# The third part of the gate-weighted one-hot rows made on ScalarE, four scaled copies per step, in a hybrid decoder layer

## The chip, the cores and the metric

One core of a Trainium2 chip runs one launch of the kernel. The metric is the device time of that launch in microseconds (us). The engines are TensorE (PE; its weight loads are shown apart as PEld), VectorE (DVE), ScalarE (ACT), GpSimd (POOL) and SyncE (SP), whose queue issues most transfers. Each engine takes its instructions in order; semaphores order them across engines.

## The reference, cut to what matters

The layer is a pooling mixer and latent attention, then a product-key expert retrieval over 128 x 128 experts for 512 tokens of width 1024. The change lies in the retrieval:

```python
s1, i1 = lax.top_k(sc[:, :, 0], PEER_TOPK)
s2, i2 = lax.top_k(sc[:, :, 1], PEER_TOPK)
cand = (s1[..., :, None] + s2[..., None, :]).reshape(TOK_CHUNK, PEER_HEADS, PEER_TOPK * PEER_TOPK)
cidx = (i1[..., :, None] * PEER_NKEYS + i2[..., None, :]).reshape(TOK_CHUNK, PEER_HEADS, PEER_TOPK * PEER_TOPK)
s, j = lax.top_k(cand, PEER_TOPK)
idx = jnp.take_along_axis(cidx, j, axis=-1)
gate = jax.nn.softmax(s, axis=-1)
u = peer_u[idx]
a = jax.nn.gelu(jnp.einsum('thkd,td->thk', u, xc).astype(jnp.float32), approximate=False)
w = (gate * a).astype(xc.dtype)
return jnp.einsum('thk,thkd->td', w, peer_v[idx])
```

Each token takes 128 experts (8 heads of 16), each named by a row number i1 and a column number i2, and weighs it by a gate.

## The kernel before, in words

The tokens are four tiles of 128. Three of them (`DT = 3`) go the dense way: for all 16384 experts, in 128 blocks of 128, the kernel forms `gelu(u x)`, multiplies by a gate matrix G that is zero for experts a token did not choose, and multiplies by v. The fourth tile gathers its experts row by row in a later stage.

G is built in the **G stage**, by `g_tiles()`. For each dense token tile `g_prep(t)` turns the list of i1, i2 and gates so that the 128 choices lie on partitions and tokens along the free axis (three PE transposes, three ScalarE copies). The gate is split into three bf16 parts, so that their sum is the fp32 gate. Then `g_tiles()` goes through the tokens four at a time: 32 steps for a token tile, 96 in all, counted by `q`. A step has these parts, in the order in which they are written:

- L1099, DVE: tile `o` of step q gets the one-hot rows of i2 and i1, for four tokens (a 128x1024 bf16 comparison).
- L1103, DVE: in the tile of step q-1, parts 2 and 3 of the output rows, as the product of the one-hot row `o[:, 1]` with two of the gate parts (128x1024 bf16).
- L1104, DVE: the same with the remaining part, in place over `o[:, 1]` (128x512 bf16).
- L1111, PE: for step q-4 (`LL = 4`), 12 matmuls of 128x128 into one PSUM tile `gp`, which has four buffers.
- L1116, ACT: for step q-5, the PSUM tile is copied to `stg`; every fourth copy is followed by a transfer to `Gd`.
- a share of `top_second(t+1)`, small DVE operations that find the choices of the next token tile (in the first two token tiles only). At step 29 of a token tile what is left of it is run out and `g_prep` of the next one follows.

Between the steps `beside()` runs `u_part()`, 2.4 times a step (`R_G` times `KD`). It makes the blocks `u x`: eight parts of three matmuls to a block (L196 to L198 in `mm3`), so a block starts every 3.33 steps. At the start of a block `u_parts()` issues the gelu of the block before (L845, ACT, waits for that block's last matmul) and then `weights()`, which splits the u block that comes next but one into a high and a low part: L208, ACT, makes the high part (128x1024), and L205, DVE, takes the difference and so waits for L208:

```python
        act.activation(hi, src, AF.Copy)
        low(lo, src, hi, eng)
```

The order on each engine is the order in which the code is written; nothing reorders it. So on DVE, L205 stands after the products of the step that has just been issued, and L1099 and L1103 of the next step stand behind it.

Of the kernel before, what the change touches and what calls it, by code (L numbers as in the profile page):

```python
# [11 lines left out]
BF = mybir.dt.bfloat16  # L12
I32 = mybir.dt.int32
U32 = mybir.dt.uint32
AF = mybir.ActivationFunctionType
# [5 lines left out]
P = 128  # L21
# [32 lines left out]
N_BACK = 36  # L54
# [95 lines left out]
def trace(ctx: ExitStack, tc: tile.TileContext, A, out):  # L150
    nc = tc.nc
    ctx.enter_context(tc.manual_schedule())
    act, dve, pe, pool, sync = nc.scalar, nc.vector, nc.tensor, nc.gpsimd, nc.sync
# [6 lines left out]
    def stage(name, space=None):  # L160
        kw = {"space": space} if space else {}
        st = stages.enter_context(ExitStack())
        return st, st.enter_context(tc.tile_pool(name=name, bufs=1, **kw))

    pools = {}
# [3 lines left out]
    BUFS = {"S2": N_S2, "F": N_F, "H": 4, "G": 2, "s": 8, "sm": 16, "sr": 1, "sa": 4}  # L169
    uid = [0]  # L170

    def T(tag, shape, dt=F32):
        uid[0] += 1
        return pools.get(tag, cpool).tile(list(shape), dt, name=f"{tag}_{uid[0]}", tag=tag, bufs=BUFS[tag])
# [4 lines left out]
    def wide(dt=F32, shape=(P, D)):  # L179
        return T("F", shape, dt)  # L180
# [90 lines left out]
    one = cpool.tile([P, 1], F32, name="one")  # L271
# [408 lines left out]
    scale = (NOPE + ROPE) ** -0.5  # L680
# [283 lines left out]
    sb_main, main = stage("sb_main")  # L964
    pools["B"] = main
    sb_top, pools["sm"] = stage("sb_top")
    pools["sm2"] = pools["gp3"] = pools["bt"] = pools["sm"]
    ps_g, psg = stage("ps_g", PSUM)
    BUFS.update(B=N_BACK, W=4, sm2=2, gp3=2, bt=2, Y=1)
    sel = {}  # L970

    def top_second(t):
# [87 lines left out]
    NQ = P // 4  # L1060
    Gd = dram.tile([P, ND // TB, NK, TB], F32, name="Gd")

    def g_prep(t):


        i1, i2, gate = sel.pop(t)
        iT, gT, gP = T("sm2", [P, NQ, 2, 4, 2], BF), T("sm", [P, P]), T("gp3", [P, NQ, 3, 4, 2], BF)
        four = lambda x: x.rearrange("p (q j) -> p q j", j=4)
        twice = lambda x: four(x).unsqueeze(3).to_broadcast([P, NQ, 4, 2])
        for x, y in ((gate, None), (i2, iT[:, :, 0]), (i1, iT[:, :, 1])):  # L1070
            uid[0] += 1
            p = psg.tile([P, S], F32, name=f"tr_{uid[0]}", tag="tr", bufs=2)[:, :P]
            pe.transpose(p, x, ident)
            if y is None:
                act.activation(gT, p, AF.Copy)
            else:
                act.activation(y, twice(p), AF.Copy)
        for n in range(3):
            dve.tensor_copy(gP[:, :, n], twice(gT))
            if n < 2:  # L1080
                dve.tensor_sub(four(gT), four(gT), gP[:, :, n, :, 0])
        return iT, gP

    def pairs(x, n):

        return x.rearrange("p a j d -> p (a j) d").unsqueeze(2).to_broadcast([P, n, P // 2, 2])

    def g_tiles():

        PB, L = TB // 4, LL  # L1090
        oo, pp, parts, stg = {}, {}, {0: g_prep(0)}, None
        rows = lambda x, n: x.rearrange("p a j (i d) -> p (a j) i d", d=2) if n else x
        iota8 = iotab.rearrange("p (i d) -> p i d", d=2).unsqueeze(1).to_broadcast([P, 8, P // 2, 2])
        for q in range(DT * NQ + L + 1):
            t, i = divmod(q, NQ)
            if t < DT:

                o = oo[q] = wide(BF, (P, 4, 4, P))
                dve.tensor_tensor(rows(o[:, :2], 8), iota8, pairs(parts[t][0][:, i], 8), op=ALU.is_equal)  # L1099
            if 1 <= q <= DT * NQ:  # L1100
                o, g = oo[q - 1], parts[(q - 1) // NQ][1][:, (q - 1) % NQ]
                one = o[:, 1:2].rearrange("p a j i -> p a (j i)").to_broadcast([P, 2, 4 * P])
                dve.tensor_mul(rows(o[:, 2:], 8), one, pairs(g[:, 1:], 8))  # L1103
                dve.tensor_mul(rows(o[:, 1:2], 4), rows(o[:, 1:2], 4), pairs(g[:, :1], 4))  # L1104
            if L <= q < DT * NQ + L:
                o = oo.pop(q - L)
                uid[0] += 1
                p = pp[q - L] = psg.tile([P, 4, P], F32, name=f"gp_{uid[0]}", tag="gp", bufs=4)
                for j in range(4):
                    for n in (2, 3, 1):  # L1110
                        pe.matmul(p[:, j], o[:, 0, j], o[:, n, j], start=n == 2, stop=n == 1)  # L1111
            if q > L:
                r = q - L - 1
                if r % PB == 0:
                    stg = T("G", [P, NK, TB])
                act.activation(stg[:, :, r % PB * 4:r % PB * 4 + 4], pp.pop(r).rearrange("p t i -> p i t"), AF.Copy)  # L1116
                if r % PB == PB - 1:
                    sync.dma_start(Gd[:, r // PB], stg)
            if t + 1 < DT:
                if i == 0:  # L1120
                    nxt, spent = top_second(t + 1), 0.0
                while spent < NTP * i:
                    spent += next(nxt, 99.0)
                if i == NQ - 1 - GP:
                    for _ in nxt:
                        pass
                    parts[t + 1] = g_prep(t + 1)
            yield KD * R_G[min(t, DT - 1)]
# [66 lines left out]
    for _ in range(NPRE2):  # L1195
        u_part()
    beside(g_tiles(), 0)
    for _ in range(N_RES):
        u_step()
# [8 lines left out]
    V, Vhl, W = {}, {}, {}  # L1208
# [125 lines left out]
```

## Time and profile before

| | us |
|---|---|
| median of 3 runs (lowest, highest) | 1620.94 (1613.51, 1621.92) |
| the profiled execution, its own time | 1618.8 |
| its span | 1616.7 |
| PE busy in the span | 1506.1 (93%) |
| DVE busy | 1299.8 (80%) |
| ACT busy | 589.7 (36%) |
| POOL busy | 469.7 (29%) |

Busy time is the sum over the span of what an engine has in work; a line number such as L1104 is that of the kernel before. The G stage lies between about 461.5 and 691.5 us of the span. In the tables of the trace a wait is put down to the instruction that released it.

### The profile page before, as it was taken

What the parts mean: (1) busy time and instruction counts of PE and PEld (TensorE: products, weight loads), DVE (VectorE), ACT (ScalarE), POOL (GpSimd) and SP (SyncE); (2) the same over time, 40 slices, a digit from 0 to 9 for tenths busy, and PEclk for the clock granted to TensorE, in tenths of its full rate; (3) what the DMA queues carried; (4) which work ended last, traced back from release to release, by engine and by line L of the source; (5) the groups of instructions that cost most, each with busy time, mean ns of one, the idle gap of its engine ahead of it and who ended that gap; (6) DMA issues with size and microseconds to landing.
All of it is one profiled execution on the core that took longest, in us unless ns stands there. A gap on an engine that the chain in (4) does not pass through costs nothing.

```text
span 1616.7 us, 22504 instructions
## 1 busy us (share of the span) xinstructions
PE 1506.1 (93%) x8153; PEld 1295.7 (80%) x8153; DVE 1299.8 (80%) x2723; ACT 589.7 (36%) x907; POOL 469.7 (29%) x341
## 2 busy tenths in 40 slices
PE   6898998899889888969999999999999999999996
PEld 4675676778877777849999888898988888898984
DVE  6877658799999898947687777687788788787697
ACT  3343442322344443423333333343333333333342
POOL 4422113333200000014334433443333233333323
PEclk9998999999999998979999999999999999999998
DMA  8554312542224344589898889889889889988881
GB/s 326 206 174 156 111 59 105 166 140 86 92 101 180 138 179 160 206 274 328 297 328 303 299 317 326 306 311 336 312 287 337 294 315 327 322 308 305 286 303 65
DMA packets 147295, 382.70 MB, mean 237 GB/s; under 512 B 11312, under 2 KB 62544, under 8 KB 144112
## 3 DMA queue, kind: packets, MB, share of 16 engines
q1 hardware_dynamic: 109328, 243.56, 43.4%
q0 software_dynamic: 37856, 137.70, 24.1%
q8 instruction: 64, 1.05, 0.3%
q14 instruction: 47, 0.39, 0.1%
HBM read 351.86 MB, written 29.36 MB: 236 GB/s over the span
## 4 chain that ended last, share of the span: by engine, by line
PE 56%; DVE 22%; DMA 2%; issue 2%; ACT 1%; POOL 0%; SPq 0%; DVEq 0%; ACTq 0%; POOLq 0%
PE acc L197 10%; PE acc L198 10%; PE acc L196 10%; PE a L196 8%; PE a L198 8%; PE a L197 8%; DVE F L1103 3%; DVE F L1099 3%; DVE F L205 2%; DVE F L1104 2%; DVE F L903 1%; DVE F L909 1%; DVE S L905 1%; PE gp L1111 1%; DMA F<-in_v,cidx 1%
## 5 line engine op out<-in xcount | busy, mean ns | idle before, releaser
L205 DVE TENSOR_TENSOR F<-F,F 128x1024 fp32r<-128x1024 f32 x255 | 314.9, 1236 | 67.2 <-ACT F L208 49.5
L196 PE MATMUL a<-H,F 128*128 128x384 f32 (+1 forms) x1040 | 361.3, 347 | 4.1 <-ACT F L208 3.2
L198 PE MATMUL a<-H,F 128*128 128x384 f32 (+1 forms) x1040 | 353.9, 340 | 6.3 <-DVE F L205 5.6
L197 PE MATMUL a<-H,F 128*128 128x384 f32 (+1 forms) x1040 | 352.6, 339 | 2.3 <-DVE H L816 2.3
L1164 POOL DMA_INDIRECT F<-in_u,cidx x128 | 169.6, 1325 | 541.0 <-PE acc L198 485.3
L196 PE MATMUL acc<-F,W 128*128 128x512 f32 x696 | 271.8, 390 | 14.9 <-ACT W L1230 14.9
L197 PE MATMUL acc<-F,W 128*128 128x512 f32 x696 | 273.4, 393 | 0.1
L198 PE MATMUL acc<-F,W 128*128 128x512 f32 x696 | 273.4, 393 | 0.0
L1164 POOL DMA_INDIRECT F<-in_v,cidx x128 | 146.8, 1147 | 274.4 <-DVE F L205 171.0
L196 PEld LDWEIGHTS a<-H,F 128*128 128x128 f32 x1040 | 198.0, 190 | 9.0 <-ACT F L208 3.5
L198 PEld LDWEIGHTS a<-H,F 128*128 128x128 f32 x1040 | 197.5, 190 | 9.4 <-DVE F L205 7.1
L197 PEld LDWEIGHTS a<-H,F 128*128 128x128 f32 x1040 | 197.9, 190 | 6.7 <-DVE H L816 2.6
L1173 DVE SCALAR_TENSOR_TENSOR F<-F,F 128x1024 f32<-128x1024 f32 x128 | 153.6, 1222 | 61.5 <-DMA F<-in_u,cidx 61.3
L1186 DVE SCALAR_TENSOR_TENSOR Y<-F,a,Y 128x1024 f32<-128x1024 f32 x127 | 162.9, 1283 | 44.9 <-DMA F<-in_v,cidx 43.4
L1228 ACT ACTIVATE F<-F 128x1024 fp32r<-128x1024 f32 x128 | 134.9, 1054 | 139.8 <-DVE F L1173 71.9
L208 ACT ACTIVATE F<-F 128x1024 fp32r<-128x1024 f32 (+2 forms) x164 | 169.5, 1036 | 42.4 <-DVE Y L1186 14.8
L196 PEld LDWEIGHTS acc<-F,W 128*128 128x128 f32 x696 | 131.4, 189 | 40.4 <-ACT W L1230 15.1
L198 PEld LDWEIGHTS acc<-F,W 128*128 128x128 f32 x696 | 131.0, 188 | 27.6 <-DVE W L205 0.2
L197 PEld LDWEIGHTS acc<-F,W 128*128 128x128 f32 x696 | 131.0, 188 | 26.2 <-DVE F L205 0.6
L845 ACT ACTIVATE B<-a 128x384 f32<-128x384 f32 x122 | 59.3, 486 | 209.7 <-PE a L198 209.6
L1230 ACT ACTIVATE W<-B 128x384 fp32r<-128x384 f32 x110 | 57.8, 525 | 213.0 <-PE acc L197 123.9
L203 POOL TENSOR_TENSOR F<-F,F 128x1024 fp32r<-128x1024 f32 (+2 forms) x37 | 84.7, 2291 | 146.5 <-ACT F L208 82.6
(290 smaller groups left out, 2108.5 us busy)
## 6 DMA issues: line engine op xcount, KB each, us to landing
F<-in_ut SPq DMA_DIRECT2D x128, 512.0 KB, 6.3
F<-in_v SPq DMA_DIRECT2D x128, 512.0 KB, 6.6
F<-in_wada SPq DMA_DIRECT2D x48, 512.0 KB, 4.3
Gd<-G SPq DMA_DIRECT2D x24, 1024.0 KB, 4.6
G<-Gd SPq DMA_DIRECT2D x15, 1536.0 KB, 13.2
F<-in_wpq SPq DMA_DIRECT2D x16, 512.0 KB, 4.3
F<-in_wout SPq DMA_DIRECT2D x8, 512.0 KB, 4.3
F<-in_win SPq DMA_DIRECT2D x8, 448.0 KB, 8.4
```

The source lines that it names most:

```text
L196: pe.matmul(o, lh, rh, start=first and i == 0, stop=False)
L197: pe.matmul(o, lh, rl, start=False, stop=False)
L198: pe.matmul(o, ll, rh, start=False, stop=last and i == n - 1)
L203: pool.tensor_sub(lo, src, f(hi))
L205: dve.tensor_sub(lo, src, f(hi))
L208: act.activation(hi, src, AF.Copy)
L845: act.activation(back[i], p, AF.Gelu)
L1164: pool.indirect_dma_start(out=g, out_offset=None, in_=table, in_offset=bass.IndirectOffsetOnAxis(ap=cidx[:, k:k + 1], axis=0))
L1173: dve.scalar_tensor_tensor(g, g, 1.0, h2r[DT], op0=ALU.mult, op1=ALU.mult, accum_out=aT[:, k:k + 1])
L1186: dve.scalar_tensor_tensor(y3, g, aT[:, k:k + 1], y3, op0=ALU.mult, op1=ALU.add)
L1228: act.activation(Vhl[j][0], v, AF.Copy)
L1230: act.activation(W[j][0], w, AF.Copy)
```

## The change

The third gate part is no longer rounded to bf16 and doubled: `g_prep` leaves the fp32 rest of the gate in `gT` and hands it on, in a tag of its own (`gr`, two buffers); one DVE cast per token tile is dropped and one subtraction of the gate stays. In `g_tiles()` the DVE product of L1104 is replaced by four ScalarE copies, one per token, each of a 128x128 bf16 block in place, with the token's column of the rest as a per-partition scale. Which gate parts lie in rows 2 and 3 changes accordingly. The steps, the matmuls and the transfers stay as they are.

```diff
-    pools["sm2"] = pools["gp3"] = pools["bt"] = pools["sm"]
+    pools["sm2"] = pools["gp3"] = pools["gr"] = pools["bt"] = pools["sm"]
...
-        iT, gT, gP = T("sm2", [P, NQ, 2, 4, 2], BF), T("sm", [P, P]), T("gp3", [P, NQ, 3, 4, 2], BF)
+        iT, gT, gP = T("sm2", [P, NQ, 2, 4, 2], BF), T("gr", [P, P]), T("gp3", [P, NQ, 2, 4, 2], BF)
...
-        for n in range(3):
+        for n in range(2):
             dve.tensor_copy(gP[:, :, n], twice(gT))
-            if n < 2:
-                dve.tensor_sub(four(gT), four(gT), gP[:, :, n, :, 0])
-        return iT, gP
+            dve.tensor_sub(four(gT), four(gT), gP[:, :, n, :, 0])
+        return iT, gP, gT
...
             if 1 <= q <= DT * NQ:
-                o, g = oo[q - 1], parts[(q - 1) // NQ][1][:, (q - 1) % NQ]
+                r = (q - 1) % NQ
+                o, (_, g, rest) = oo[q - 1], parts[(q - 1) // NQ]
                 one = o[:, 1:2].rearrange("p a j i -> p a (j i)").to_broadcast([P, 2, 4 * P])
-                dve.tensor_mul(rows(o[:, 2:], 8), one, pairs(g[:, 1:], 8))
-                dve.tensor_mul(rows(o[:, 1:2], 4), rows(o[:, 1:2], 4), pairs(g[:, :1], 4))
+                dve.tensor_mul(rows(o[:, 2:], 8), one, pairs(g[:, r], 8))
+                for j in range(4):
+                    act.activation(o[:, 1, j], o[:, 1, j], AF.Copy, scale=rest[:, 4 * r + j:4 * r + j + 1])
```

Lines move by one or two: in the changed kernel the two-part product is L1104, the four copies are L1106, the matmuls L1113 and the PSUM copy L1118, while L205, L208, L845 and L1099 keep their numbers.

The order on ScalarE, at the start of one u block in the first token tile. A G name is the staging tile, gp a PSUM tile, F a tile of the wide ring (an `o`, a u block or its parts), gr the fp32 rest; what an instruction waits for stands in brackets. Before:

```order
L1116 ACTIVATE G_4287<-gp_4244 128x128x4 [waits PE_49]
L1116 ACTIVATE G_4287<-gp_4274 128x128x4 [waits PE_49]
L845 ACTIVATE B_4323<-a_4210 128x384 [waits PE_49]
L208 ACTIVATE F_4327<-F_4111 128x1024 [waits DMAHW7_49]
L1116 ACTIVATE G_4287<-gp_4306 128x128x4 [waits PE_49]
L1116 ACTIVATE G_4287<-gp_4342 128x128x4 [waits PE_49]
```

And in the changed kernel at the same place:

```order
L1106 ACTIVATE F_4293<-F_4293,gr_4033 128x128 [waits DVE_49,PE_49,Activation_49]
L1106 ACTIVATE F_4293<-F_4293,gr_4033 128x128 x3
L1118 ACTIVATE G_4313<-gp_4300 128x128x4
L845 ACTIVATE B_4352<-a_4227 128x384 [waits PE_49]
L208 ACTIVATE F_4356<-F_4119 128x1024 [waits DMAHW7_49]
L1106 ACTIVATE F_4328<-F_4328,gr_4033 128x128 [waits DVE_49]
L1106 ACTIVATE F_4328<-F_4328,gr_4033 128x128 x3
L1118 ACTIVATE G_4313<-gp_4335 128x128x4 [waits PE_49]
```

Before, ScalarE waited at this place for PE and a transfer alone. Now a group of copies that waits for VectorE stands ahead of each PSUM copy, and one stands right behind L208; that is so at 27 blocks of the G stage.

The order on VectorE at the same block (sm, s and bt are the small tiles of `top_second`). Before:

```order
L1099 TENSOR_TENSOR F_4302<-iotab,sm_683_4032 128x1024
L1103 TENSOR_TENSOR F_4270<-F_4270,gp_685_4034 128x1024
L1104 TENSOR_TENSOR F_4270<-F_4270,gp_685_4034 128x512 [waits DVE_49]
L1022 TENSOR_TENSOR sm_4320<-sm_4070,s_4290 128x8x16
L1028 TENSOR_SCALAR bt_4261<-sm_4259 128x256
L205 TENSOR_TENSOR F_4328<-F_4111,F_4327 128x1024 [waits DMAHW7_49,PE_49,Activation_49]
L1099 TENSOR_TENSOR F_4338<-iotab,sm_683_4032 128x1024
L1103 TENSOR_TENSOR F_4302<-F_4302,gp_685_4034 128x1024
```

And in the changed kernel:

```order
L1099 TENSOR_TENSOR F_4328<-iotab,sm_683_4032 128x1024 [waits PE_49]
L1104 TENSOR_TENSOR F_4293<-F_4293,gp_685_4034 128x1024
L1022 TENSOR_TENSOR sm_4349<-sm_4072,s_4316 128x8x16 [waits DVE_49]
L1028 TENSOR_SCALAR bt_4284<-sm_4282 128x256
L205 TENSOR_TENSOR F_4357<-F_4119,F_4356 128x1024 [waits DMAHW7_49,Activation_49]
L1099 TENSOR_TENSOR F_4367<-iotab,sm_683_4032 128x1024 [waits PE_49]
L1104 TENSOR_TENSOR F_4328<-F_4328,gp_685_4034 128x1024 [waits DVE_49]
```

One product per step is gone from VectorE. The copies of F_4328 that stand behind L208 on ScalarE need the last of these rows, and that stands behind L205 on VectorE, which needs F_4356 of that same L208.

## Rows read from the trace of the kernel before

**Rows 1.** Busy time by stretch, inside and over the G stage (columns in the first line)
```profile
core 0: us, PE busy (x) PEld busy (x) DVE busy (x) ACT busy (x) POOL busy (x), PEclk, DMA share, GB/s
...
614.00:620.00 6.00, 3.75 (x15) 3.45 (x16) 5.76 (x16) 1.15 (x3) 0.00 (x0) 0.50 0.24 87
620.00:665.00 45.00, 45.00 (x433) 41.54 (x431) 39.98 (x67) 21.47 (x36) 0.00 (x0) 0.98 0.56 188
...
sum 230.00, PE 202.19 PEld 178.25 DVE 215.51 ACT 100.27 POOL 0.00; mean PE 33.70 PEld 29.71 DVE 35.92 ACT 16.71 POOL 0.00
```
**Rows 2.** Waits in the G stage: who waited for whom, us in total, times, longest
```profile
ACT G L1116 <- PE gp L1111: 61.6, 49, 3.2
ACT B L845 <- PE a L198: 42.7, 25, 2.7
...
PE tr L1073 <- DVE sm L1054: 13.8, 2, 6.9
...
DVE F L205 <- ACT F L208: 8.8, 4, 4.1
```
**Rows 3.** Groups by line, G stage: count, busy us, mean ns, idle before them
```profile
L1116 ACT ACTIVATE G<-gp 128x512 f32<-128x512 f32 x96 | 55.9, 597 | 66.7 <-PE gp L1111 61.6 <-ACT G L1116 3.0 <-issue 1.4
...
L1104 DVE TENSOR_TENSOR F<-F,gp 128x512 bf16<-128x512 bf16 x96 | 40.8, 425 | 3.3
L205 DVE TENSOR_TENSOR F<-F,F 128x1024 fp32r<-128x1024 f32 x28 | 34.3, 1225 | 8.8 <-ACT F L208 8.8
L208 ACT ACTIVATE F<-F 128x1024 fp32r<-128x1024 f32 x28 | 29.4, 1050 | 0.0
L845 ACT ACTIVATE B<-a 128x384 f32<-128x384 f32 x27 | 13.3, 491 | 42.7 <-PE a L198 42.7
L979 ACT ACT_TABLE_LOAD x2 | 2.6, 1283 | 0.0
...
L1079 DVE CAST gp<-sm 128x256 bf16<-128x256 f32 x7 | 2.0, 292 | 0.2
```
**Rows 4.** Timeline of VectorE, third token tile: start us, duration us, engine, line, operation
```profile
645.50 1.22 DVE L205 TENSOR_TENSOR F<-F,F 128x1024 fp32r<-128x1024 f32 x1
646.63 0.69 DVE L1099 TENSOR_TENSOR F<-iotab,sm 128x1024 bf16<-128x1024 bf16 x1
647.23 0.69 DVE L1103 TENSOR_TENSOR F<-F,gp 128x1024 bf16<-128x1024 bf16 x1
647.95 0.42 DVE L1104 TENSOR_TENSOR F<-F,gp 128x512 bf16<-128x512 bf16 x1
648.30 0.69 DVE L1099 TENSOR_TENSOR F<-iotab,sm 128x1024 bf16<-128x1024 bf16 x1
```
**Rows 5.** Timeline of ScalarE, the same token tile
```profile
650.05 0.49 ACT L845 ACTIVATE B<-a 128x384 f32<-128x384 f32 x1 [2.29 <-PE a L198]
650.44 1.05 ACT L208 ACTIVATE F<-F 128x1024 fp32r<-128x1024 f32 x1
651.39 1.07 ACT L1116 ACTIVATE G<-gp 128x512 f32<-128x512 f32 x2
```
**Rows 6.** Timeline of ScalarE, before the G stage: eight 128x128 activations in a row
```profile
239.70 2.90 ACT L814 ACTIVATE F<-ps,modc 128x128 f32<-128x128 f32 x8 [4.60 <-PE ps L810]
```
**Rows 7.** Groups by line and shape on ScalarE, whole span
```profile
L814 ACT ACTIVATE F<-ps,modc 128x128 f32<-128x128 f32 x32 | 11.6, 468 | 8.1 <-PE ps L810 7.3 <-issue 0.8
...
L712 ACT ACTIVATE G<-ps 128x128 f32<-128x128 f32 x6 | 1.6, 269 | 0.0
...
L593 ACT ACTIVATE S<-ps,gc 128x512 fp32r<-128x512 f32 x2 | 1.4, 687 | 0.4 <-PE ps L590 0.4
...
L604 ACT ACTIVATE S<-a 128x512 f32<-128x512 f32 x2 | 1.2, 598 | 2.2 <-PE a L198 2.1
```
**Rows 8.** Timeline across a wait: ScalarE's split, VectorE's difference
```profile
536.86 1.05 ACT L208 ACTIVATE F<-F 128x1024 fp32r<-128x1024 f32 x1
...
537.94 1.23 DVE L205 TENSOR_TENSOR F<-F,F 128x1024 fp32r<-128x1024 f32 x1 [1.75 <-ACT F L208]
```
**Rows 9.** Busy time in a stretch before the G stage (columns as in Rows 1)
```profile
272.00:276.00 4.00, 1.54 (x7) 1.29 (x8) 3.93 (x5) 0.00 (x0) 3.00 (x2) 1.00 0.15 60
```

More of the change, by code (lines that the diff above doesn't have):

```diff
@@ L966, in trace @@
     sb_top, pools["sm"] = stage("sb_top")
-    pools["sm2"] = pools["gp3"] = pools["bt"] = pools["sm"]
+    pools["sm2"] = pools["gp3"] = pools["gr"] = pools["bt"] = pools["sm"]
     ps_g, psg = stage("ps_g", PSUM)
-    BUFS.update(B=N_BACK, W=4, sm2=2, gp3=2, bt=2, Y=1)
+    BUFS.update(B=N_BACK, W=4, sm2=2, gp3=2, gr=2, bt=2, Y=1)
     sel = {}
```

## The prediction

> **What bounds the kernel now.** The change touches the G stage alone, so I read that stage and not the averages of the span. First busy time by stretch: in the stage's 230.0 us VectorE is busy for 215.5, TensorE for 202.2, ScalarE for 100.3 [rows 1]. Then the waits: ScalarE waits for TensorE (61.6 us at L1116, 42.7 at L845), while VectorE waits almost for nobody, for ScalarE's split in 4 places of 28 with 8.8 us in all [rows 2]. The reader should see an order of lead in this: VectorE's line is full, TensorE has done all that VectorE's products let it do, and ScalarE, which waits for TensorE, is as far ahead. Since L208 was done long before VectorE comes to L205, that pair costs VectorE only its own 1.13 us (start to start, [rows 4]). By this reading less work on VectorE should pay and work on ScalarE should be free. What decides is whether ScalarE can keep its lead when its work needs VectorE's.
>
> **What is removed.** L1104, 96 times. It lasts 0.42 us, but the next instruction starts 0.35 us after it [rows 4], so 96 x 0.35 = 34 us of VectorE's line go. The 128x256 cast goes three times at 0.29 us [rows 3], 0.9 us, one of them before the stage. A VectorE step without `top_second` falls from 1.67 us (648.30 less 646.63) to 1.32 [rows 4]. `top_second` and the like take what is left of VectorE's busy time: 215.5 - 96 x 1.67 - 28 x 1.13 = 23.6 us, over some 60 steps 0.39 us each. So the step becomes 1.32 + 0.39 = 1.71 us in the first two token tiles and 1.32 in the third.
>
> **What is added.** 384 copies on ScalarE, 128x128 bf16 with one per-partition scale. No row shows this form. The nearest is L814, 128x128 with two per-partition operands: 468 ns each, but eight in 2.90 us, so one starts (2.90 - 0.468)/7 = 0.347 us after the other [rows 6, 7]. One such operand adds 687 - 598 = 89 ns to a 128x512 activation [rows 7]. Less one operand the spacing is 0.26 us, which I take. Bounds: below, the 269 ns of a copy without one [rows 7] less the overlap of 0.12 us of L814, 0.15; above, 0.47, L814 with no overlap. A step's four copies take 1.04 us of ScalarE's line.
>
> The Trainium skill, page "ScalarE: Activation LUTs", section "What ACT_TABLE_LOAD costs", gives 186 ns plus 0.833 ns per element for an activation, 93 ns for each per-partition operand, and an overlap of 93 ns back to back. By it a copy would take 0.293 us of the line, an estimate, and the sum below would be 384 x 0.033 = 13 us higher, about 1682 us. The trace agrees on the operand (89 ns) and shows a little more overlap.
>
> **What is moved: who leads.** The copies of step q-1 stand ahead of the next gelu and split on ScalarE, and they need the product that VectorE has just made. So ScalarE can no longer be ahead of VectorE. At each u block VectorE ends that product, has one step's `top_second` left, and stops at L205 until ScalarE has done four copies, a PSUM copy, L845 and L208. Behind L208 ScalarE's next instruction is again a group of copies, which needs L205, L1099 and L1104 of the changed kernel to pass on VectorE. The two engines take turns: a round trip per block, at 27 blocks.
>
> - The trip, ScalarE idle: L205 to product's end is 647.23 + 0.69 - 645.50 = 2.42 us [rows 4]. A hop between the engines is 537.94 - (536.86 + 1.05) = 0.03 us [rows 8]; two make 2.49 us with rounding.
> - The same stop on VectorE: 1.04 + 0.47 + 0.39 + 1.05 = 2.95 us less 0.39 of `top_second`. (0.47 is the second of two PSUM copies in 1.07 us, the first of 0.60; L845 to L208 is 0.39, L208 lasts 1.05 [rows 3, 5].)
>
> TensorE is not in the way: its products of step q-4 are ready three steps before, and its 202.2 us for 28 blocks, 7.2 each, stand against some 10 for a block below. GpSimd does nothing in the stage and SyncE's transfers keep their places; their buffers come free later, as everything does.
>
> **The sum**, as ScalarE's line through the stage:
>
> - copies 384 x 0.26 = 99.8
> - PSUM copies 96 x 0.47 = 45.1
> - gelus and splits 28 x (0.39 + 1.05) = 40.3
> - round trips 27 x 2.49 = 67.2
> - four table loads, two for the exponential and two back, of 1.283 us [rows 3], hidden before by ScalarE's lead: 5.1
> - ScalarE's step of 1.51 us is shorter than VectorE's 1.71 in the first two token tiles; the last step of each of 19 blocks is covered by the trip, so (64 - 19) x 0.20 = 9.0
> - two changes of token tile: three copies, four VectorE operations of 0.29 us, then 1.3 us to the next product, estimated at 4 us each: 8.0
> - start and end: some 3 us to the first product, five PSUM copies after the last: 6
>
> That is 280.5 us against 230.0: 50 us more. What follows the stage moves with it. The profiled execution took 1618.8 us, 2.1 below the median of the runs; on it the sum gives **1669 us**, 3% slower. By the lower bound of a copy, VectorE's steps bind and 27 trips shorten by 0.44 us each: some 16 us less, 1653. By the upper one 81 more less the 9: 1741.
>
> **The rivals.**
>
> - *ScalarE keeps its lead, VectorE's relief pays* (the other side). If L208 were done before VectorE gets to L205, ScalarE's 100 + 100 us would fit, VectorE's line would fall to 182, and TensorE would be the bound: 202.2 busy plus the 13.8 us of its two waits at the token tiles [rows 1, 2], 216 us, 14 less: 1605 us. It decides from the point where VectorE's stop at L205 is under a third of a microsecond. For it: the averages, and 24 of 28 splits without a wait now. Against it: the order of both engines, where copies that need VectorE stand ahead of each split. Chance 0.08.
> - *The copies don't overlap* (each waits for the one before, or for a semaphore): 0.47 us or so, 1741 us. L814 speaks against it, though it isn't in place. Chance 0.06.
> - *TensorE's clock falls.* With TensorE idle for about 2.5 us in each block, the granted clock could go to 1.2 GHz: after a wait of 6.9 us it was 0.50 in the next stretch [rows 1, 2]. A block would take TensorE 14.4 us instead of 7.2, 4.5 above the 9.9 of a block: 28 x 4.5 = 126 us if it always stays low, 42 for a third of the blocks, 1711 us. Against it: with 1.54 us busy in 4 the clock was 1.00 in an earlier stretch [rows 9]. Chance 0.05.
>
> That the copies are not made at all is excluded by the order on ScalarE, which lists them.
>
> **How the numbers follow.** The forecast has the rest, 0.81. Its own spread comes from the copy's price (0.2 to 0.35 us), the estimated ends and hops, and trips that are partly covered: 1638 to 1705. That leaves out the faster rival, the copies without overlap and the worse half of the clock, under 2 in 10, so it is the range. Half a per cent, 8 us, is about what can be told from no change here. Faster by more than that has 0.08, from the first rival; within it 0.03, the low tail of the forecast; slower 0.89.
>
> **What the changed profile would show.** Right: VectorE waiting for ScalarE at L205 some 27 times for about 2.6 us, near 70 us in all; ScalarE waiting for VectorE at the copies as often and as long; ScalarE busy for about 200 us of a stage of about 280, VectorE for about 180; TensorE's waits grown by 50 us or so; the stages behind unchanged in length. The mean of a copy should read 0.35 to 0.40 us. Wrong: no wait at L205 and a stage of 216 us; or a stage of 280 us with ScalarE full and no trips, which would mean a dear copy and not an exchange of turns; or a granted clock of 0.5 across the stage.

## The result and the profile after

The changed kernel takes 1678.01 us (median of four runs, 1674.26 to 1679.03) against 1619.93 us before: a ratio of 1.0365 with a 95% interval of 1.0337 to 1.0393. It is slower by 58 us; 1669 us, in a range of 1638 to 1705, had been forecast. The profiled execution took 1674.26 us, its span is 1672.4 us.

First, busy time by stretch of the changed kernel, with the columns of [rows 1]: what lies ahead of the G stage, the stage, and what lies behind it.

```profile
0.00:461.50 461.50, 407.70 (x1932) 318.88 (x1933) 375.40 (x1395) 164.05 (x303) 136.95 (x78) 0.95 0.43 144
...
461.50:748.00 286.50, 220.94 (x1831) 198.90 (x1829) 177.47 (x316) 208.62 (x549) 0.00 (x0) 0.89 0.39 133
...
748.00:1672.40 924.40, 896.17 (x4392) 798.59 (x4392) 709.39 (x914) 323.74 (x439) 328.11 (x263) 0.98 0.86 301
```

The last stretch took 925.2 us before and takes 924.4 now, so the whole loss is in the stage: 286.5 us against 230.0. In it ScalarE went from 100.3 us busy to 208.6 and VectorE from 215.5 to 177.5; both are now far from full. The waits say what they do in between, the counterpart of [rows 2] (us in total, times, longest):

```profile
DVE F L205 <- ACT F L208: 98.3, 28, 6.5
ACT F L1106 <- DVE F L1104: 74.2, 30, 2.6
...
ACT B L845 <- PE a L198: 1.5, 1, 1.5
```

Each of the two waits for the other, once in every u block, and ScalarE's waits for TensorE, 104 us before, are gone but for 1.5: its lead is lost. Of ScalarE's 30 waits, 28 last 2.50 to 2.56 us and stand one behind each split L208, 70.9 us in all; the other two, of 1.66 us, stand at the changes of token tile. The groups by line, as in [rows 3], give the copy's own price:

```profile
L1106 ACT ACTIVATE F<-F,gr 128x128 bf16<-128x128 bf16 x384 | 122.2, 391 | 75.3 <-DVE F L1104 74.2 <-PE gp L1113 0.4
...
L205 DVE TENSOR_TENSOR F<-F,F 128x1024 fp32r<-128x1024 f32 x28 | 34.3, 1226 | 98.3 <-ACT F L208 98.3
L208 ACT ACTIVATE F<-F 128x1024 fp32r<-128x1024 f32 x28 | 29.5, 1054 | 0.0
```

And one turn, from the timelines of ScalarE and then of VectorE of the changed kernel (start us, duration us; idle time and releaser in brackets at the end):

```profile
481.42 0.47 ACT L845 ACTIVATE B<-a 128x384 f32<-128x384 f32 x1
481.79 1.05 ACT L208 ACTIVATE F<-F 128x1024 fp32r<-128x1024 f32 x1
485.39 1.31 ACT L1106 ACTIVATE F<-F,gr 128x128 bf16<-128x128 bf16 x4 [2.56 <-DVE F L1104]
486.61 0.57 ACT L1118 ACTIVATE G<-gp 128x512 f32<-128x512 f32 x1
487.12 1.28 ACT L1106 ACTIVATE F<-F,gr 128x128 bf16<-128x128 bf16 x4
488.31 0.58 ACT L1118 ACTIVATE G<-gp 128x512 f32<-128x512 f32 x1
488.90 1.28 ACT L1106 ACTIVATE F<-F,gr 128x128 bf16<-128x128 bf16 x4
```

```profile
482.87 1.23 DVE L205 TENSOR_TENSOR F<-F,F 128x1024 fp32r<-128x1024 f32 x1 [2.87 <-ACT F L208]
484.01 0.69 DVE L1099 TENSOR_TENSOR F<-iotab,sm 128x1024 bf16<-128x1024 bf16 x1
484.61 0.68 DVE L1104 TENSOR_TENSOR F<-F,gp 128x1024 bf16<-128x1024 bf16 x1
...
486.35 0.68 DVE L1104 TENSOR_TENSOR F<-F,gp 128x1024 bf16<-128x1024 bf16 x1
...
488.11 0.68 DVE L1104 TENSOR_TENSOR F<-F,gp 128x1024 bf16<-128x1024 bf16 x1
```

L208 ends at 482.84, and VectorE, idle for 2.87 us, starts L205; ScalarE then stands idle for 2.56 us until the product of L1104 ends at 485.29.

### The profile page after: what moved, and what is told of

It is laid out like the page before. It is cut to its first block, busy times and chain, and to the rows that moved or that the text cites. A ratio compares the mean times of both kernels' runs of the same rounds, so it can differ in the third digit from the quotient of the medians.

```text
span 1672.4 us, 22862 instructions
## 1 busy us (share of the span) xinstructions
PE 1524.8 (91%) x8153; PEld 1316.4 (79%) x8153; DVE 1262.3 (75%) x2624; ACT 696.4 (42%) x1291; POOL 465.1 (28%) x341
## 3 DMA queue, kind: packets, MB, share of 16 engines
q0 software_dynamic: 37856, 137.70, 23.1%
## 4 chain that ended last, share of the span: by engine, by line
PE 53%; DVE 17%; ACT 11%; issue 2%; DMA 1%; SPq 0%; ACTq 0%; DVEq 0%
PE acc L197 10%; PE acc L198 10%; PE acc L196 10%; PE a L198 8%; PE a L196 8%; PE a L197 7%; ACT F L1106 6%; DVE F L205 3%; ACT G L1118 2%; ACT F L208 2%; DVE F L1104 1%; DVE F L1099 1%; DVE F L909 1%; DVE F L903 1%; DVE S L905 1%
## 5 line engine op out<-in xcount | busy, mean ns | idle before, releaser
L205 DVE TENSOR_TENSOR F<-F,F 128x1024 fp32r<-128x1024 f32 x255 | 314.8, 1235 | 164.8 <-ACT F L208 139.5
L196 PE MATMUL a<-H,F 128*128 128x384 f32 (+1 forms) x1040 | 367.1, 353 | 4.1 <-ACT F L208 3.2
L198 PE MATMUL a<-H,F 128*128 128x384 f32 (+1 forms) x1040 | 359.0, 345 | 8.8 <-DVE F L205 6.6
L197 PE MATMUL a<-H,F 128*128 128x384 f32 (+1 forms) x1040 | 357.5, 344 | 2.3 <-DVE H L816 2.3
L1166 POOL DMA_INDIRECT F<-in_u,cidx x128 | 162.6, 1270 | 605.2 <-PE acc L198 547.0
L198 PEld LDWEIGHTS a<-H,F 128*128 128x128 f32 x1040 | 201.5, 194 | 12.9 <-DVE F L205 9.5
L196 PEld LDWEIGHTS a<-H,F 128*128 128x128 f32 x1040 | 202.3, 195 | 9.4 <-ACT F L208 3.8
L197 PEld LDWEIGHTS a<-H,F 128*128 128x128 f32 x1040 | 202.0, 194 | 6.6 <-DVE H L816 2.6
L208 ACT ACTIVATE F<-F 128x1024 fp32r<-128x1024 f32 (+2 forms) x164 | 169.7, 1036 | 41.0 <-DVE Y L1188 14.1
L1106 ACT ACTIVATE F<-F,gr 128x128 bf16<-128x128 bf16 x384 | 122.2, 391 | 75.3 <-DVE F L1104 74.2
L1113 PE MATMUL gp<-F 128*128 128x128 bf16 x1152 | 91.4, 234 | 49.7 <-ACT G L1118 25.6
```

The source lines that it names most:

```text
L196: pe.matmul(o, lh, rh, start=first and i == 0, stop=False)
L197: pe.matmul(o, lh, rl, start=False, stop=False)
L198: pe.matmul(o, ll, rh, start=False, stop=last and i == n - 1)
L205: dve.tensor_sub(lo, src, f(hi))
L1106: act.activation(o[:, 1, j], o[:, 1, j], AF.Copy, scale=rest[:, 4 * r + j:4 * r + j + 1])
L1166: pool.indirect_dma_start(out=g, out_offset=None, in_=table, in_offset=bass.IndirectOffsetOnAxis(ap=cidx[:, k:k + 1], axis=0))
```

## The experiments

The theory: the loss is a matter of order. Copies that stand at step q-1 need VectorE's newest product, L205 needs ScalarE's newest split, and so the two engines take turns once a block. The rival: ScalarE is full, and copies on it are simply too dear. A third candidate is TensorE's clock, 0.89 in the stage. All ratios are against the kernel before, on the same chip.

**Taking the dependence away, and the work.** In the first run the copies keep their place on ScalarE but read a constant and write a spare tile. The edit is against the kernel before:

```diff
-                dve.tensor_mul(rows(o[:, 1:2], 4), rows(o[:, 1:2], 4), pairs(g[:, :1], 4))
+                for j in range(4):
+                    act.activation(spare[:, j], iotab, AF.Copy, scale=cst[:, 4 * ((q - 1) % NQ) + j:4 * ((q - 1) % NQ) + j + 1])
```

(So it keeps the third cast of the kernel before, 0.9 us, and a ring of small tiles that is two shorter. In this run and the next the row `o[:, 1]` goes into the matmul unscaled.)

> The changed kernel with the four copies still on ScalarE at the same place in its order, but reading a constant and writing a spare tile, so that they wait for no VectorE product and nobody waits for them; the third gate part is left out of G. Theory (turns: the 50 to 60 us are 27 round trips between L208 and the next copies): ScalarE keeps its lead, no wait of VectorE at L205 beyond some 10 us, the stage is bound by TensorE at about 216 us, total 1600 to 1615 us. Rival (ScalarE is simply full, the copies are too dear): the same copies cost the same, total 1660 us or more.

1594.8 us, ratio 0.986 (0.983 to 0.989), a little under the range of the theory. ScalarE has as much to do as in the changed kernel, 202.6 us, and fits it into a stage of 210 us. The stage's stretch, and the line of the copies:

```profile
463.80:673.80 210.00, 193.43 (x1824) 176.73 (x1822) 176.33 (x315) 202.58 (x547) 0.00 (x0) 0.98 0.52 181
...
L1106 ACT ACTIVATE spare<-iotab,cst 128x128 bf16<-128x128 bf16 x384 | 125.9, 437 | 0.0
```

No idle time stands before the copies. The rival falls: ScalarE's work fits into 210 us, so its amount does not make a stage of 286.5. VectorE still waits 29.0 us at L205, more than the 10 expected; the next run shows that most of this is not the copies' doing.

The second run drops the copies:

> The changed kernel without the four copies: the third gate part is left out of G, VectorE's product is gone and ScalarE gets nothing. It gives the most that taking the product off VectorE can be worth. Turns: 1600 to 1610 us, the stage at TensorE's floor of about 216 us, and within 8 us of the run with free copies. Rival (ScalarE full): 1605 us here, 50 us or more under the run with free copies.

1585.6 us, ratio 0.982 (0.978 to 0.985), lower than I had thought possible. Its stage, and three of its waits:

```profile
459.00:659.50 200.50, 192.23 (x1826) 177.07 (x1825) 175.05 (x313) 99.54 (x164) 0.00 (x0) 0.97 0.54 192
...
ACT B L845 <- PE a L198: 42.8, 25, 2.3
DVE F L205 <- ACT F L208: 21.7, 11, 4.6
...
PE tr L1074 <- DVE sm L1054: 7.4, 2, 4.1
```

So the product's removal is worth 32 us by itself, and the free copies take 9 of them. With nothing added to ScalarE, VectorE waits 21.7 us at L205 here too: the split stands behind a gelu, and the gelu waits for TensorE. TensorE, busy for 192.2 us and waiting for 7.4, fills this stage of 200.5 us.

**Changing the order alone.** The third run does the whole computation and moves the copies two steps:

```diff
+            if CL <= q < DT * NQ + CL:
+                r, rest = (q - CL) % NQ, parts[(q - CL) // NQ][2]
+                o = oo[q - CL]
                 for j in range(4):
                     act.activation(o[:, 1, j], o[:, 1, j], AF.Copy, scale=rest[:, 4 * r + j:4 * r + j + 1])
```

with `CL = 3`.

> The changed kernel with its copies two steps later in the order: at step q they work on the tile of step q-3 and not q-1, whose product VectorE made two steps before; the matmuls stay at q-4. The result is the whole one. Turns: behind L208 ScalarE finds copies whose product is done, so the 27 waits of 2.5 us at the copies go; VectorE's wait at L205 falls under 30 us; the stage is ScalarE's line without trips, 114 + 45 + 40 + 5 and some 14 us of ends, 215 to 235 us; total 1605 to 1625 us. Rival (ScalarE full): 1660 us or more. Rival (TensorE now has only one step between copies and matmuls and is what waits): 1630 to 1650 us, with TensorE's waits at the copies.

1598.1 us, ratio 0.988 (0.985 to 0.991), under the range expected. This is below both kernels: by the two ratios some 78 us under the changed one, by order alone, and 1.2% under the one before. Its stage and its waits, and ScalarE's timeline behind a split (here L209 is the split and L1110 the copies):

```profile
463.50:674.00 210.50, 199.00 (x1827) 178.63 (x1825) 176.04 (x313) 203.31 (x548) 0.00 (x0) 0.98 0.53 183
...
DVE F L206 <- ACT F L209: 27.3, 20, 4.6
...
PE gp L1117 <- ACT F L1110: 3.7, 8, 1.1
```

```profile
490.43 1.08 ACT L209 ACTIVATE F<-F 128x1024 fp32r<-128x1024 f32 x1
491.38 1.29 ACT L1110 ACTIVATE F<-F,gr 128x128 bf16<-128x128 bf16 x4
492.55 0.61 ACT L1122 ACTIVATE G<-gp 128x512 f32<-128x512 f32 x1
```

The copies start while the split's tail still runs; ScalarE's 74.2 us of waits for the product (L1104, here L1105) are gone from the list. That is the theory shown: the same instructions without the turn. Four copies take as long as before, 1.17 us to the start of the PSUM copy (491.38 to 492.55), against 1.22 and 1.19 in the turn above.

**How many steps it takes.** The same with `CL = 2`:

> As the run with copies two steps later, but only one step later: at step q the copies work on the tile of step q-2. Turns: one step is enough, since the product of q-2 stands on VectorE ahead of the L205 that waits for the split, so ScalarE finds it done behind L208; 1595 to 1608 us, ScalarE's wait at the copies under 10 us in all. Rival (what helped was slack of two steps in general, not the undoing of the turn): half way, 1630 to 1650 us.

1623.7 us, ratio 1.004 (1.003 to 1.005): between the expected range and the rival's, so my view that one step is enough was wrong, and the timelines of both engines show why.

```profile
496.28 1.05 ACT L209 ACTIVATE F<-F 128x1024 fp32r<-128x1024 f32 x1
497.23 1.27 ACT L1110 ACTIVATE F<-F,gr 128x128 bf16<-128x128 bf16 x4
498.40 0.58 ACT L1122 ACTIVATE G<-gp 128x512 f32<-128x512 f32 x1
499.89 1.27 ACT L1110 ACTIVATE F<-F,gr 128x128 bf16<-128x128 bf16 x4 [0.91 <-DVE F L1105]
```

```profile
497.37 1.23 DVE L206 TENSOR_TENSOR F<-F,F 128x1024 fp32r<-128x1024 f32 x1 [1.34 <-ACT F L209]
498.51 0.68 DVE L1100 TENSOR_TENSOR F<-iotab,sm 128x1024 bf16<-128x1024 bf16 x1
499.11 0.68 DVE L1105 TENSOR_TENSOR F<-F,gp 128x1024 bf16<-128x1024 bf16 x1
```

The first group of copies behind the split finds its product done. It and the PSUM copy last until 498.98, but VectorE, which restarted at the split's end, has its next product only at 499.79. The turn costs ScalarE 0.91 us here and not 2.5 (23.1 us in 26 waits in all, most of the 26 us that this run is slower than the one with two steps). VectorE's stop at the split is 54.7 us in all, between the 98.3 of the changed kernel and the 27.3 with two steps. Two steps of distance give it two groups of copies to do meanwhile, and that covers the trip.

**Is it TensorE?** With the copies two steps later, the matmuls were moved one step on (`LL = 5`):

> Copies two steps later, and the matmuls five steps behind the comparison instead of four, so that a copy has two steps until its matmul. ScalarE's line bounds the stage: no change against the run with matmuls at four, within 6 us of 1598. Rival (TensorE's slack behind the copies bounds it): 8 us or more faster.

1598.9 us, ratio 0.988 (0.986 to 0.990): no change, as expected. That TensorE has only one step between the copies and its matmuls does not set the pace.

**Other cures.** The difference L205 on GpSimd instead of VectorE, copies at q-1 (`ueng[:] = [pool]` ahead of the stage, `[dve]` behind it):

> The changed kernel with the difference L205 of the G stage's u blocks on GpSimd, which does nothing in the stage; the copies stay at step q-1. Turns: VectorE no longer stops for L208, so both halves of the turn go; ScalarE's line is 218 us without trips and VectorE's 150 us; stage 215 to 235 us, total 1605 to 1625 us, with GpSimd busy 28 times for about 2.3 us. Rival (ScalarE full): 1660 us or more.

1616.5 us, ratio 1.000 (0.999 to 1.001), as expected. The loss is gone, though ScalarE has as much to do as in the changed kernel (203.4 us busy): its wait at the copies falls from 74.2 to 23.4 us. What keeps a gain from showing came in with GpSimd: a difference takes 2.74 us there, VectorE stands idle for 34.5 us ahead of L1099, for TensorE and GpSimd, and its instructions take longer on average, L1099 847 ns where it was 685. The groups of this run by line:

```profile
L1099 DVE TENSOR_TENSOR F<-iotab,sm 128x1024 bf16<-128x1024 bf16 x95 | 80.5, 847 | 34.5 <-PE gp L1113 14.2 <-PE a L198 7.4 <-POOL F L203 6.5
...
L203 POOL TENSOR_TENSOR F<-F,F 128x1024 fp32r<-128x1024 f32 x28 | 76.7, 2739 | 182.2 <-ACT F L208 165.5 <-DVE F L1104 7.4 <-PE gp L1113 4.8
L1104 DVE TENSOR_TENSOR F<-F,gp 128x1024 bf16<-128x1024 bf16 x96 | 74.1, 772 | 0.0
```

The other half of the turn, the split L208, on GpSimd (`pool.tensor_copy(hi, src)` in `split` during the stage), once with the copies at q-1 and once two steps later:

> The changed kernel, copies at step q-1, with the high part L208 of the u blocks in the G stage made on GpSimd instead of ScalarE; VectorE's difference stays. GpSimd needs nothing of ScalarE or VectorE for it, only the loaded block, so it can be done early. Turns: VectorE's wait at L205 goes (under 15 us) and with it the wait of ScalarE at the copies; ScalarE's line loses 28 us of splits and is about 180 us, VectorE's 180 us; total 1590 to 1605 us, at or under the run with copies two steps later. Rival (ScalarE follows VectorE in any case and its order at q-1 is what costs): 1625 us or more, with ScalarE's waits at the copies above 40 us and each of them dear. Rival (GpSimd's copy is slow or holds up VectorE): VectorE waits at L205 for GpSimd, 1610 to 1640 us.

> High part on GpSimd and the copies two steps later. If ScalarE's full line (207 us busy) is what is left over the run without a third part (1585.6 us), taking 28 us off it gives 1586 to 1594 us. Rival (VectorE or TensorE bounds the stage with copies two steps later): 1596 to 1600 us, no change against it.

With the copies at q-1: 1607.2 us, ratio 0.994 (0.992 to 0.996), by the ratios some 69 us under the changed kernel. ScalarE's wait at the copies falls from 74.2 to 30.5 us with the copies where the change put them, so breaking the turn at the split works too. But it is not a clean second proof, since the 29.5 us of splits have left ScalarE's line as well: some 44 us are the turn's and the rest is work taken away. The run with the difference on GpSimd, which leaves ScalarE its work, is the cleaner one. The expected 1605 was missed by little; VectorE waits for GpSimd in 13 places instead (18.8 us, 15 having been expected at most). With both: 1602.6 us, ratio 0.990 (0.988 to 0.993), whose interval overlaps that of the copies alone: nothing gained. This came out as neither side expected, and it does not clear ScalarE's line of being what is left over, since VectorE now waits 18.0 us for GpSimd and its products are busy for 70.4 us where they were 65.7. The product's row in this run:

```profile
L1110 DVE TENSOR_TENSOR F<-F,gp 128x1024 bf16<-128x1024 bf16 x96 | 70.4, 734 | 0.0
```

**Sharing the row.** Copies two steps later for three tokens, and the fourth scaled on VectorE (shown against the run with four); then two and two:

```diff
+                for j in range(3, 4):
+                    dve.tensor_scalar(o[:, 1, j], o[:, 1, j], rest[:, 4 * r + j:4 * r + j + 1], None, op0=ALU.mult)
...
-                for j in range(4):
+                for j in range(3):
```

> Copies two steps later for three of the four tokens; the fourth token's block is scaled on VectorE, in place, with the same per-partition scale. If ScalarE's line (207 us busy of a stage of some 212) is now the bound, it falls by 96 x 0.297 = 28 us while VectorE's grows by 96 x 0.15 = 14 to about 194: 1585 to 1594 us. Rival (VectorE or TensorE bounds it): 1598 us or slower.

> The same with two tokens on each engine: ScalarE 150 us, VectorE about 208 of the stage. VectorE is then the fuller engine again: 1590 to 1602 us, slower than with three and one. Rival (VectorE's small operations are hidden): at or under the run with three and one.

1606.4 us (0.993, 0.991 to 0.995) and 1616.6 us (1.000, 0.999 to 1.002): both slower than four copies, and both outside what I expected. In the first it is the rival that came out, VectorE or TensorE as the bound. VectorE's timeline with three and one:

```profile
640.16 0.68 DVE L1105 TENSOR_TENSOR F<-F,gp 128x1024 bf16<-128x1024 bf16 x1
640.88 0.26 DVE L1107 TENSOR_SCALAR F<-F,gr 128x128 bf16<-128x128 bf16 x1
641.05 0.68 DVE L1100 TENSOR_TENSOR F<-iotab,sm 128x1024 bf16<-128x1024 bf16 x1
641.65 0.69 DVE L1105 TENSOR_TENSOR F<-F,gp 128x1024 bf16<-128x1024 bf16 x1
```

The step is 1.49 us where it is 1.21 with four copies. I had counted 0.15 for the small product. It writes in place what the product before it reads, and it starts 0.72 us after that product, where the comparison's successor starts after 0.60; L1104 of the kernel before, in place too, also started 0.72 us after its product [rows 4]. With that the small product costs 0.28. 96 x 0.28 is 27 us, about what ScalarE was to gain, and VectorE, with a longer line, makes ScalarE wait again (20.0 us at the copies).

## Why the prediction was right

The direction, the place and the mechanism were as forecast, and 58 us stand against a forecast of 50. Step by step:

- **Who leads.** Read from the order of both engines and the small waits of [rows 2], against the busy shares. It is what decided: the waits came at 28 blocks on VectorE and behind 28 splits on ScalarE, 27 trips having been forecast.
- **The trip.** 2.49 us forecast, 2.50 to 2.56 in the timelines; 67.2 us in all against 70.9 measured. The 28th is the wait for the first product, which the sum had under the start.
- **The copy.** This term was undersized. Four take 1.28 us and one lasts 0.39, so the spacing is (1.28 - 0.39)/3 = 0.297 us, not 0.26: 14 us more over 384. I had subtracted a whole operand from L814's spacing, and L814 reads PSUM where the copies read SBUF; no run parts these two. The price of the Trainium skill ("ScalarE: Activation LUTs", "What ACT_TABLE_LOAD costs"), 0.293 as an estimate, fits the trace, and the total by it, 1682 us, was nearer to the measured 1678.
- **The stage.** 280.5 us forecast, 286.5 measured. ScalarE's own work was 190.3 in the sum (copies, PSUM copies, gelus, splits, table loads) and is 208.6; its idle time was 90 in the sum and is 78. Of the work that was missed the copies are 14 us. Of the idle time that did not come, 8 are the term for VectorE's longer step: 9.0 in the sum, about 1 in the timeline, because with dearer copies ScalarE's step is as long as VectorE's. The ends and changes of token tile, 14 in the sum, were too long as well. So the total is closer than its terms: errors cancelled, and that part is luck.
- **VectorE's step.** 1.71 us forecast for the first two token tiles; its products there start 1.76 us apart (486.35, 488.11).
- **VectorE's stop at L205** was forecast at 2.6 us each, near 70 in all, and is 98.3, 3.5 each. Its own step is shorter than ScalarE's in the third token tile, so that it arrives earlier and stops longer, and the table loads lie in it (longest 6.5). It costs nothing more, since ScalarE sets the end.
- **The first rival's price.** ScalarE keeping its lead was to give 1605 us. The run without a third part gives 1585.6: TensorE's 202 us of busy time and 13.8 of waits were not its floor. In that run the same products show 192.2 us busy and 7.4 of waits. Their records are as long on average (221 ns for the G matmul in both), so in the kernel before they overlapped less, as they would when they come with gaps between them. The rival did not happen, but the gain it named is real and larger than I thought.
- **The clock.** It did fall, to 0.89 over the stage. It costs nothing that a run shows: ScalarE waited for TensorE once, for 1.5 us, and the clock is back at 0.98 as soon as the order is changed.

What stays open: why the copies two steps later end 12.5 us above the run without a third part. The free copies show 9 of them, and ScalarE's line of 203 us in a stage of 210 is the likeliest bound. But taking work off it did not help: the splits on GpSimd and the tokens scaled on VectorE each made VectorE's line longer in the same run. The runs do not part the two.

## What to carry to other kernels

A busy share tells whether an engine has room, not whether work may be moved there: look at which engine leads, and whether the moved work makes the leader wait for the follower. If the two already hand something over in the other direction, each hand-over becomes a round trip with both idle. Before giving such a move up, put some steps of distance between producer and consumer: here two steps turned a loss of 3.6% into a gain of 1.2% with the same instructions.

## What was not expected of the hardware

Some of VectorE's products stall when GpSimd works beside them. The mean of the 128x1024 bf16 product is 685 ns with GpSimd idle, 734 with 28 casts on GpSimd around the stage, and 772 with 28 differences there. But its median stays at 682 to 685 ns, and what grows is the longest, from 691 ns in the changed kernel to 1547 with the casts and 2889 with the differences: most products are not touched and a few are held up, by up to 0.9 and 2.2 us. The Trainium skill, "SBUF — State Buffer", section "SBUF: two separate sides", says that the two share one pair of ports under an exclusive lock; the rows agree with that, and no run here shows the lock itself. And a 128x128 in-place product of 0.26 us cost VectorE 0.28 us a step, more than its own length, because it started 0.12 us later behind its product than an independent successor does.
